# One queue for loads and stores: moving seven stores from ScalarE's DMA queue to SP's in a 1D Lp pooling kernel

## The chip, the cores and the metric

The kernel runs on one core of one Trainium2 chip. The metric is the device time of one execution in microseconds (us). All runs quoted are of state fast, and the granted clock was 1.00 in all of them.

Some words used throughout:

- A *load* brings x into on-chip memory, a *store* writes results back. Both are DMA transfers of 128 rows.
- A transfer is carried out by 16 DMA engines, 8 rows each. The trace records every row (here called a row or packet) with start and duration, and for each transfer 16 completions, one per DMA engine. The Trainium skill, page "DMA: Bandwidth & Descriptors", section "Why a DMA increments its semaphore by 16 and not by 1", says that the participating engines finish independently and that only the full 16 mean that all data has landed.
- A *ring* is what one DMA engine works off, in order, for one queue. The *lag* of a transfer is the last of its 16 completions minus the first. It is worked out from the trace's completion records, not printed by any view.
- A *slot* is a buffer of x; "slot 17's load" is the load of the eighteenth slot. A *turn* is the place in a ring where a store follows a load.

DVE is VectorE, ACT is ScalarE, POOL is GpSimd, SP is SyncE. A q after an engine's name means its sequencer, which issues transfers.

## The reference

```python
x: (32, 256, 4096) float32, p = 2.0, kernel_size = 4
for i in range(out_length):
    window = np.abs(x[:, :, 4*i:4*i+4]) ** p
    result[:, :, i] = np.mean(window, axis=-1) ** (1.0 / p)
```

With p = 2 this is the square root of the mean of four neighbouring squares. 134.22 MB are read and 33.55 MB written.

## The kernel before

All data is treated as one flat array, cut into rows over 128 partitions. Three slots for x (52,736 bytes per partition each) and two output buffers (26,368 bytes) rotate. Each of the groups 0 to 8 is two slots (groups 9 and 10 share the last two); the result of a group is one store. ScalarE squares a chunk, VectorE sums groups of four, ScalarE takes the root of the chunk before.

```python
    W, O_W = 13184, 6592
    X_SLOTS, O_SLOTS = 3, 2
    slots = [[(W, [4416, 4384, 4384])]] * 18
    slots += [[(6592, [3296, 3296])] * 2, [(6592, [3296, 3296]), (5056, [2528, 2528])]]
    groups = [2] * 9 + [3, 1]
    late = {7, 8, 9, 10}          # stored at the end, by SP
    in_x = {9, 10}                # these results go to a free slot of x
    # ... cut: bookkeeping, load(i) issues nc.sync.dma_start ...

    def store(g, queue):
        queue.dma_start(out=block(of, g, k), in_=ots[g])

    def root(g, o, ends):
        nc.scalar.activation(out=o, in_=o, func=Act.Sqrt, scale=1.0 / k)
        if ends and g not in late:
            store(g, nc.scalar)   # groups 0 to 6
    # ... cut ...
    for i in range(n):
        s, _, w, chunks = loads[i]
        while ahead < n and loads[ahead][0] < s + X_SLOTS:
            load(ahead)           # two slots ahead of the compute
            ahead += 1
        # ... cut: tiles ...
        for step in chunks:
            nc.scalar.activation(out=v, in_=v, func=Act.Square)
            nc.vector.tensor_reduce(out=o, in_=v.rearrange("p (n j) -> p n j", j=k), ...)
            if pending is not None:
                root(*pending)
            # ... cut ...
    for g in sorted(late):
        store(g, nc.sync)
```

Of the kernel before, what the change touches and what calls it, by code (L numbers as in the profile page):

```python
# [1 line left out]

# [4 lines left out]


@with_exitstack
def kernel(  # L10
    ctx: ExitStack,
    tc: tile.TileContext,
    x: bass.AP,
    p: float,
    kernel_size: int,
    out: bass.AP,
):






    nc = tc.nc

    assert float(p) == 2.0, "kernel specialized for p == 2"
    k = int(kernel_size)
    assert k == 4, "kernel specialized for kernel_size == 4"

    P = nc.NUM_PARTITIONS  # L30
    fp32 = mybir.dt.float32
    Act = mybir.ActivationFunctionType
    xf = x.rearrange("b c l -> (b c l)")
    of = out.rearrange("b c l -> (b c l)")
    total = xf.shape[0] // P
# [5 lines that stand above are left out]
    groups = [2] * 9 + [3, 1]  # L41
    late = {7, 8, 9, 10}
    in_x = {9, 10}


    loads = [(s, sum(w for w, _ in slot[:j]), *slot[j]) for s, slot in enumerate(slots)
             for j in range(len(slot))]
    n = len(loads)
    assert sum(w for _, _, w, _ in loads) == total

    firsts = [sum(groups[:g]) for g in range(len(groups))]
    assert sum(groups) == n
    group_of = [g for g, count in enumerate(groups) for _ in range(count)]
    columns = [sum(w for _, _, w, _ in loads[firsts[g]:firsts[g] + groups[g]])
               for g in range(len(groups))]

    x_pool = ctx.enter_context(tc.tile_pool(name="x_pool", bufs=X_SLOTS))
    o_pool = ctx.enter_context(tc.tile_pool(name="o_pool", bufs=O_SLOTS))
    ctx.enter_context(tc.manual_schedule())

    def block(flat, g, div):
        at, width = sum(columns[:g]) * P // div, columns[g] * P // div
        return flat[at:at + width].rearrange("(p w) -> p w", p=P)

    slot_tiles = {}
    xs = {}

    def load(i):
        s, at, w, _ = loads[i]
        if at == 0:  # L70
            slot_tiles[s] = x_pool.tile([P, W], fp32, name="xt")
        v = slot_tiles[s][:, at:at + w]
        g = group_of[i]
        src = sum(loads[j][2] for j in range(firsts[g], i))
        nc.sync.dma_start(out=v, in_=block(xf, g, 1)[:, src:src + w])  # L75
        xs[i] = v

    ots = {}

    def store(g, queue):  # L80
        queue.dma_start(out=block(of, g, k), in_=ots[g])  # L81

    def root(g, o, ends):
        nc.scalar.activation(out=o, in_=o, func=Act.Sqrt, scale=1.0 / k)  # L84
        if ends and g not in late:
            store(g, nc.scalar)

    ahead = 0
    while ahead < n and loads[ahead][0] < X_SLOTS - 1:
        load(ahead)  # L90
        ahead += 1
    pending = None
    for i in range(n):
        s, _, w, chunks = loads[i]
        while ahead < n and loads[ahead][0] < s + X_SLOTS:
            load(ahead)
            ahead += 1
        g = group_of[i]
        if i == firsts[g]:
            pool, width = (o_pool, O_W) if g not in in_x else (x_pool, W)  # L100
            t = pool.tile([P, width], fp32, name="ot" if g not in in_x else "xt")
            ots[g] = t[:, 0:columns[g] // k]
        at = sum(loads[j][2] for j in range(firsts[g], i)) // k
        assert sum(chunks) == w
        c = 0
        for step in chunks:
            v = xs[i][:, c:c + step]
            nc.scalar.activation(out=v, in_=v, func=Act.Square)  # L108
            o = ots[g][:, at + c // k:at + (c + step) // k]
            nc.vector.tensor_reduce(  # L110
                out=o, in_=v.rearrange("p (n j) -> p n j", j=k),
                axis=mybir.AxisListType.X, op=mybir.AluOpType.add,
            )
            if pending is not None:
                root(*pending)
            c += step
            pending = (g, o, i == firsts[g] + groups[g] - 1 and c == w)
    root(*pending)
    for g in sorted(late):
        store(g, nc.sync)  # L120


# [1 line left out]
_INS = ['x', 'p', 'kernel_size']  # L124
_OUTS = [((32, 256, 1024), 'float32')]

_NUMBERS = {'p': 2.0, 'kernel_size': 4}


# [26 lines left out]
```

## Time and profile before

| | before |
|---|---|
| time, median of 6 runs | 394.80 us (394.69 to 395.12) |
| span of the profiled run | 393.0 us |
| DVE / ACT busy | 72% / 74% |
| DMA, two queues together | 99.3% of 16 engines' span |
| row of a load / of a store | 1,947 ns / 978 ns (median of the row records) |

Lines of the page of the kernel before. The DMA line gives tenths of busy time in 40 slices of the span; a queue line gives packets, MB and the share of sixteen engines' span. The line of the sums ends with DVE's idle time before them; the last two give the transfers of one kind, KB each, and the median us from issue to landing.

```profile
span 393.0 us, 316 instructions
DVE 282.4 (72%) x62; ACT 292.4 (74%) x126; POOL 0.2 (0%) x4
...
DMA  8999999999999999999999999999999999999997
...
q1 hardware_dynamic: 3744, 144.15, 85.3%
q10 hardware_dynamic: 1008, 23.63, 14.0%
...
DMA 62%; ACT 19%; DVE 14%; issue 2%; ACTq 0%; SPq 0%
...
L110 DVE TENSOR_REDUCE ot<-xt 128x1096 f32<-128x4384 f32 (+1 forms) x54 | 255.4, 4731 | 102.7 <-ACT xt L108 102.4
...
xt<-in_x_dram SPq DMA_DIRECT2D x18, 6592.0 KB, 39.7
out_dram<-ot ACTq DMA_DIRECT2D x7, 3296.0 KB, 26.4
```

No compute engine is near full, and the DMA engines are full from the first microseconds to the last: the kernel is bound by DMA. Queue q1 is SP's (loads and the four late stores), q10 ScalarE's (seven stores).

Who waits for whom, in the kernel before (total us, times, longest):

```profile
DVE ot L110 <- ACT xt L108: 102.4, 36, 23.4
...
ACT xt L108 <- DMA xt<-in_x_dram: 86.3, 18, 17.5
```

Compute waits for loads only, never for a store. In the timeline, at slot 4 and at the end (start, duration, engine, line, operation):

```profile
90.41 3.88 ACT L108 ACTIVATE xt<-xt 128x4416 f32<-128x4416 f32 x1 [4.84 <-DMA xt<-in_x_dram]
94.32 4.75 DVE L110 TENSOR_REDUCE ot<-xt 128x1104 f32<-128x4416 f32 x1 [5.01 <-ACT xt L108]
...
339.75 3.88 ACT L108 ACTIVATE xt<-xt 128x4416 f32<-128x4416 f32 x1 [1.07 <-DMA xt<-in_x_dram]
...
381.39 6.11 SPq L81 DMA_DIRECT2D out_dram<-xt  x2
...
386.42 0.73 ACT L84 ACTIVATE xt<-xt 128x632 f32<-128x632 f32 x1 [2.23 <-DVE xt L110]
```

Slot 4's load has landed by 90.4 us, slot 17's by 339.75 us; from there ACT and DVE run almost without a break to 387 us, and the last two stores are issued at 381.4 and 387.2 us.

### The profile page before, as it was taken

How to read it: one execution, taken by the hardware profiler on the slowest of the kernel's cores; microseconds unless marked ns; L12 is line 12 of the kernel's file. 1: busy time of each engine (PE TensorE's matmuls, PEld its weight loads, DVE VectorE, ACT ScalarE, POOL GpSimd, SP SyncE). 2: the span in 40 equal slices, each digit the busy share in tenths (PEclk: the TensorE clock that was granted, in tenths of full speed). 3: DMA queues.
4: the chain of work that ended last, by engine and by line, in shares of the span. 5: the costliest groups of instructions: out<-in, count | busy, mean ns of one | idle time of the engine just before them, and what ended most of it. 6: DMA issues, size and time to landing. Idle time of an engine off the chain costs nothing.

```text
span 393.0 us, 316 instructions
## 1 busy us (share of the span) xinstructions
DVE 282.4 (72%) x62; ACT 292.4 (74%) x126; POOL 0.2 (0%) x4
## 2 busy tenths in 40 slices
DVE  0068989494959495949594959595859686899992
ACT  1099986777786768686958695959595949899991
POOL 0000000000000000000000000000000000000000
DMA  8999999999999999999999999999999999999997
GB/s 344 429 429 440 429 424 381 443 459 429 413 440 435 429 427 432 429 440 441 437 448 421 432 462 435 392 429 472 429 413 451 425 429 429 424 429 427 438 429 329
DMA packets 4754, 167.79 MB, mean 427 GB/s; under 512 B 528, under 2 KB 528, under 8 KB 656
## 3 DMA queue, kind: packets, MB, share of 16 engines
q1 hardware_dynamic: 3744, 144.15, 85.3%
q10 hardware_dynamic: 1008, 23.63, 14.0%
q14 instruction: 2, 0.02, 0.0%
HBM read 134.22 MB, written 33.55 MB: 427 GB/s over the span
## 4 chain that ended last, share of the span: by engine, by line
DMA 62%; ACT 19%; DVE 14%; issue 2%; ACTq 0%; SPq 0%
DMA xt<-in_x_dram 62%; ACT xt L108 15%; DVE ot L110 11%; DVE xt L110 3%; ACT ot L84 3%; ACT xt L84 1%; ACTq L81 0%; SPq L75 0%; ACTq L108 0%
## 5 line engine op out<-in xcount | busy, mean ns | idle before, releaser
L110 DVE TENSOR_REDUCE ot<-xt 128x1096 f32<-128x4384 f32 (+1 forms) x54 | 255.4, 4731 | 102.7 <-ACT xt L108 102.4
L108 ACT ACTIVATE xt<-xt 128x4384 f32<-128x4384 f32 (+3 forms) x62 | 230.3, 3716 | 89.2 <-DMA xt<-in_x_dram 86.3
L84 ACT ACTIVATE ot<-ot 128x1096 f32<-128x1096 f32 (+1 forms) x54 | 59.8, 1108 | 1.8 <-DVE ot L110 0.9
L110 DVE TENSOR_REDUCE xt<-xt 128x824 f32<-128x3296 f32 (+1 forms) x8 | 27.0, 3384 | 1.3 <-ACT xt L108 1.2
L84 ACT ACTIVATE xt<-xt 128x824 f32<-128x824 f32 (+1 forms) x8 | 6.7, 841 | 3.0 <-DVE xt L110 2.9
L108 ACT ACT_TABLE_LOAD x1 | 1.3, 1283 | 0.7 <-PEq L137 0.7
L84 ACT ACT_TABLE_LOAD x1 | 1.3, 1283 | 0.0
L137 POOL MEMSET const-bfloat16-1.0<- 128x1 bf16 x1 | 0.1, 101 | 0.0
L137 POOL MEMSET const-uint8-127<- 128x1 uint8 x1 | 0.1, 101 | 0.0
L137 POOL MEMSET const-float32-0.0<- 128x1 f32 x1 | 0.1, 98 | 0.2 <-issue 0.2
L137 POOL MEMSET const-float32-1.0<- 128x1 f32 x1 | 0.1, 98 | 0.0
## 6 DMA issues: line engine op xcount, KB each, us to landing
xt<-in_x_dram SPq DMA_DIRECT2D x18, 6592.0 KB, 39.7
out_dram<-ot ACTq DMA_DIRECT2D x7, 3296.0 KB, 26.4
xt<-in_x_dram SPq DMA_DIRECT2D x3, 3296.0 KB, 24.6
out_dram<-ot SPq DMA_DIRECT2D x2, 3296.0 KB, 29.6
xt<-in_x_dram SPq DMA_DIRECT2D x1, 2528.0 KB, 26.4
out_dram<-xt SPq DMA_DIRECT2D x1, 2472.0 KB, 9.3
out_dram<-xt SPq DMA_DIRECT2D x1, 632.0 KB, 5.0
```

The costliest lines, as they stand in the source:

```text
L84: nc.scalar.activation(out=o, in_=o, func=Act.Sqrt, scale=1.0 / k)
L108: nc.scalar.activation(out=v, in_=v, func=Act.Square)
L110: nc.vector.tensor_reduce(out=o, in_=v.rearrange("p (n j) -> p n j", j=k), axis=mybir.AxisListType.X, op=mybir.AluOpType.add,)
L137: nc = _bacc.Bacc("TRN2", target_bir_lowering=False, num_devices=1)
```

## The change

The intent is to issue all stores from SP's queue, in turn with the loads, and none from ScalarE. The rewritten bookkeeping (FINE, LAG) at the values given here leaves the order of the squares, sums and roots as it was. What is left of the change is one word:

```diff
@@
     in_x = {9, 10}
+    FINE, LAG = 0, 1
@@
         nc.scalar.activation(out=o, in_=o, func=Act.Sqrt, scale=1.0 / k)
         if ends and g not in late:
-            store(g, nc.scalar)
+            store(g, nc.sync)
@@ (cut: the same passes, with a list of pending roots)
+            while pending and pending[0][0] <= done - LAG:
+                root(*pending.pop(0)[1:])
```

In SP's order a store now stands behind the load of two slots ahead: load, load, store, load, load, store.

More of the change, by code (lines that the diff above doesn't have):

```diff
@@ L85, in root, with total_sum @@
         if ends and g not in late:
-            store(g, nc.scalar)
+            store(g, nc.sync)
+    def total_sum(o, v, i):
+        nc.vector.tensor_reduce(
+            out=o, in_=v.rearrange("p (n j) -> p n j", j=k),
+            axis=mybir.AxisListType.X, op=mybir.AluOpType.add,
+        )
     ahead = 0
@@ L91 @@
         ahead += 1
-    pending = None
+    pending = []
+    done = 0
     for i in range(n):
@@ L102 @@
             ots[g] = t[:, 0:columns[g] // k]
-        at = sum(loads[j][2] for j in range(firsts[g], i)) // k
+            summed = rooted = 0
         assert sum(chunks) == w
@@ L108 @@
             nc.scalar.activation(out=v, in_=v, func=Act.Square)
-            o = ots[g][:, at + c // k:at + (c + step) // k]
-            nc.vector.tensor_reduce(
-                out=o, in_=v.rearrange("p (n j) -> p n j", j=k),
-                axis=mybir.AxisListType.X, op=mybir.AluOpType.add,
-            )
-            if pending is not None:
-                root(*pending)
-            c += step
-            pending = (g, o, i == firsts[g] + groups[g] - 1 and c == w)
-    root(*pending)
+            total_sum(ots[g][:, summed:summed + step // k], v, i)
+            while pending and pending[0][0] <= done - LAG:
+                root(*pending.pop(0)[1:])
+            done += 1
+            c += step
+            summed += step // k
+            ends = summed == columns[g] // k
+            if ends or i >= FINE:
+                pending.append((done - 1, g, ots[g][:, rooted:summed], ends))
+                rooted = summed
+    for job in pending:
+        root(*job[1:])
     for g in sorted(late):
```

## The prediction

> **What bounds the kernel now.** The DMA engines. In the page's slices the DMA row reads 9 nearly everywhere; DVE is busy 72% and ACT 74% of the span. The queue lines give 85.3% (loads and last stores) plus 14.0% (ScalarE's stores) = 99.3% of sixteen engines' span of 393.0 us. In the packet records one engine's packets sum to 390.1 us; the first starts at 1.7 us, the last ends at 391.7: no gaps. A load row (52,736 bytes) takes 1,947 ns and a store row (26,368 bytes) 978 ns, alone or beside the other queue: sharing costs no bandwidth. The chain of waits agrees: 62% DMA loads.
>
> **What the change does.** The order of ACT's and DVE's passes stays. It removes seven store issues from ACT (0.34 us each, on an engine 26% idle) and adds them to SP, each behind the load two slots ahead. No load should wait behind a store: each store is ready before the next load in SP's order, whose slot still has reductions to run.
>
> What moves is the order inside the rings. Before, store and load rows alternate when both queues hold work (the Trainium skill, "DMA: Bandwidth & Descriptors", section Queues, rings and completion order: round-robin at packet granularity); 26 us from issue to landing for a store that needs 7.8 us alone (8 x 978 ns) agrees. After, one ring runs in order: load, load, store. My estimate from 15.6 us per load and 7.8 per store: the first load of a group lands about 8 us earlier (slot 4 near 82 us instead of 90.4), the store behind it near 90. Stores take 34 to 43 us to land instead of 26.
>
> With two output buffers, the first reduction of group g waits for the store of g-2. Now the load comes last; after, the store: DVE waits for it some 4 us after the first squaring, seven times. But that reduction starts 3 to 4 us earlier than now (about 90.4 against 94.3 in slot 4), since load plus store are the same bytes. Loads keep their lead: each is issued some 20 us before its turn.
>
> **The tail.** Bytes ahead of slot 17's load are the same, so it lands near 339.7 us as now; slot 16 is reduced some 4 us earlier. From there ACT and DVE run without a break to 387 us, and the four late stores stay on SP. Group 9's store is issued at 381.4, the one before lands at 384.8: about a microsecond to spare after start-up, a little more after. The end stays with the rings.
>
> **Predicted time.** Head 1.7 + packets 390.1 + landing and end 1.2 = 393.0 us of span, 394.7 us measured (now 394.79). There is nothing to win; only a gap could cost. Range 394.1 to 396.0. Faster by over 2%: 0.01, within 2%: 0.96, slower by over 2%: 0.03.
>
> **What would show each step.** Queue 1 carries all 167.8 MB at 99%; packet times unchanged; store issue to landing about 40 us; DVE's or ACT's idle before the first chunk of groups 2 to 8 ends with a store; load issue to landing 35 to 40 us; no wait of SP for a store's data that empties the ring.
>
> **What would make it wrong.** A gap in the ring at each change from load to store (at 1 us each, up to 14 us); a waiting store holding a load until the ring runs dry; slot 16's reduction gated so late by group 6's store that the compute tail outlasts the stores: several us more.

## The result, and the profile after

| | before | after |
|---|---|---|
| time, median of 6 runs | 394.80 us (394.69 to 395.12) | 397.11 us (396.80 to 397.23) |
| ratio | | 1.0057, 95% interval 1.0044 to 1.0070 |
| span of the profiled run | 393.0 us | 395.3 us |
| mean of the 16 rings' packet time | 390.1 us | 390.7 us |
| end of the last packet | 391.7 us | 394.0 us |
| lag of slot 17's load | 0.94 us | 3.34 us |

A ratio is the mean time of one kernel's fast runs over that of the other's fast runs of the same rounds, so it is not quite the ratio of the medians quoted.

The change costs 2.3 us (0.6%): within 2%, but outside the predicted range (394.1 to 396.0), and clear of the noise.

Lines of the page after:

```profile
span 395.3 us, 330 instructions
DVE 281.7 (71%) x62; ACT 291.8 (74%) x126; POOL 0.2 (0%) x4
...
DMA  8999999989999999999999999999999999999996
...
q1 hardware_dynamic: 4752, 167.77, 98.8%
...
DMA 67%; ACT 15%; DVE 15%; issue 0%; SPq 0%; DVEq 0%; ACTq 0%
...
L90 DVE TENSOR_REDUCE ot<-xt 128x1096 f32<-128x4384 f32 (+1 forms) x54 | 254.7, 4729 | 105.7 <-ACT xt L116 67.0
...
xt<-in_x_dram SPq DMA_DIRECT2D x18, 6592.0 KB, 37.4
out_dram<-ot SPq DMA_DIRECT2D x9, 3296.0 KB, 41.8
```

There is one queue now. The DMA line looks full as before, with an 8 near 80 us and a 6 at the end. Stores take 41.8 us to land instead of 26.4, since they queue behind two loads.

The waits after (the last line is of SP's own waits, shown by a view of its own):

```profile
DVE ot L90 <- ACT xt L116: 67.0, 29, 23.6
ACT xt L116 <- DMA xt<-in_x_dram: 64.4, 18, 17.7
DVE ot L90 <- DMA out_dram<-ot: 38.7, 7, 6.6
...
SPq L76 <- DVE ot L90: 292.2, 17, 18.6
```

A new wait stands here: seven times DVE waits for a store to free the output buffer. It is tempting to call these 38.7 us the cause. But 102.4 us of waiting for ACT became 67.0 (and the wait of ACT for loads fell from 86.3 to 64.4): DVE's idle time before these sums is 105.7 us after against 102.7 before. The timeline shows the same:

```profile
83.68 3.88 ACT L116 ACTIVATE xt<-xt 128x4416 f32<-128x4416 f32 x1 [2.57 <-DMA xt<-in_x_dram]
91.51 4.75 DVE L90 TENSOR_REDUCE ot<-xt 128x1104 f32<-128x4416 f32 x1 [6.65 <-DMA out_dram<-ot]
...
326.55 9.38 DVE L90 TENSOR_REDUCE ot<-xt 128x1104 f32<-128x4416 f32 x2 [5.43 <-DMA out_dram<-ot]
...
342.07 3.88 ACT L116 ACTIVATE xt<-xt 128x4416 f32<-128x4416 f32 x1 [4.85 <-DMA xt<-in_x_dram]
...
383.73 6.12 SPq L82 DMA_DIRECT2D out_dram<-xt  x2
...
388.75 0.73 ACT L85 ACTIVATE xt<-xt 128x632 f32<-128x632 f32 x1 [2.23 <-DVE xt L90]
```

In slot 4 the sum starts at 91.5 us, earlier than before (94.3). But slot 17 starts at 342.07 instead of 339.75 us, 2.3 us later, behind a load, and everything after it is later by the same amount.

The completions tell why. First and last of the 16 completions (us), from the trace's records:

```
                       before                    after
slot 4's load       89.55   90.38 (0.83)      81.57   83.60 (2.03)
slot 6's load      128.47  129.32 (0.86)     120.52  123.07 (2.54)
slot 8's load      167.39  168.24 (0.85)     159.47  162.40 (2.94)
slot 12's load     245.24  246.06 (0.82)     237.43  240.32 (2.89)
slot 17's load     338.72  339.67 (0.94)     338.64  341.99 (3.34)
store of group 8   383.81  384.76            383.74  387.07
store of group 9   389.70  390.66            390.84  392.97
store of group 10  391.25  392.22            392.39  394.53
```

The first ring to complete slot 17's load is as early as before (338.64 against 338.72); the last is 2.3 us later. At the end, the last completions follow one another at 5.90 and 1.56 us, which is 8 rows of 735 ns and 8 of 194 ns: the ring that is last works without a pause. The first completions of groups 8 and 9 are 7.10 us apart where 8 rows need 5.88: those rings had run dry, because the next store was not yet issued (383.73 us, when the first ring was already done with group 8's). So the sixteen rings have drifted apart, and the end is set by the one that is last.

The row records show where. Of the rows of 1,947 ns that start after 50 us, those stretched by more than 100 ns are, after the change: 17 at 77.8 to 80.3 us, directly ahead of the first store, and one at 91.1 (16.9 us of stretch together, about 1 us for every ring); then 25 more in small sets of 1 to 8 to the end, all but three of them just before one of the stores 1 to 6 begins (7.9 us together, up to 0.83 us in one row). Before the change there are 29 between 56 and 62 us, at the first store (15.7 us together, again about 1 us per ring), and then two in the whole rest. These two (at 178.0 and 310.3 us), and two of the three exceptions after the change (175.0 and 307.8), start as a packet of 309 ns of queue q14, named "instruction" on the page, ends. Such a pair stands in both kernels, so it does not explain their difference.

### The profile page after: what moved, and what is told of

It reads as the page before. It is cut to its first block, busy times and chain, and to the rows that moved or that the text cites. A ratio compares the mean times of both kernels' runs of the same rounds, so it can differ in the third digit from the quotient of the medians.

```text
span 395.3 us, 330 instructions
## 1 busy us (share of the span) xinstructions
DVE 281.7 (71%) x62; ACT 291.8 (74%) x126; POOL 0.2 (0%) x4
## 3 DMA queue, kind: packets, MB, share of 16 engines
q1 hardware_dynamic: 4752, 167.77, 98.8%
## 4 chain that ended last, share of the span: by engine, by line
DMA 67%; ACT 15%; DVE 15%; issue 0%; SPq 0%; DVEq 0%; ACTq 0%
DMA xt<-in_x_dram 46%; DMA out_dram<-ot 21%; ACT xt L116 12%; DVE ot L90 12%; DVE xt L90 3%; ACT ot L85 2%; ACT xt L85 1%; SPq L76 0%; DVEq L90 0%; ACTq L116 0%
## 5 line engine op out<-in xcount | busy, mean ns | idle before, releaser
L90 DVE TENSOR_REDUCE ot<-xt 128x1096 f32<-128x4384 f32 (+1 forms) x54 | 254.7, 4729 | 105.7 <-ACT xt L116 67.0
L116 ACT ACTIVATE xt<-xt 128x4384 f32<-128x4384 f32 (+3 forms) x62 | 230.3, 3716 | 64.4 <-DMA xt<-in_x_dram 64.4
## 6 DMA issues: line engine op xcount, KB each, us to landing
xt<-in_x_dram SPq DMA_DIRECT2D x18, 6592.0 KB, 37.4
out_dram<-ot SPq DMA_DIRECT2D x9, 3296.0 KB, 41.8
```

## The experiments

*Theory A*: at a turn from a load to a store inside one ring, load rows in flight are stretched, not equally in all rings; a ring that falls behind never catches up, because it is never idle; the last ring sets the landing of slot 17's load and the end. *Rivals*: B, one event at the first store; C, with two queues the rings even out again; D, the waits for output buffers (compute); E, the compute tail that starts late, rather than the ring.

Every kernel was run in 5 rounds against the kernel before on the same chip; there were two chips, one for d_one, d_two, e_tail_light and e_warm_before, the other for the rest. Each run's lag is that of its one profiled execution. Where two queues are at work, the lag of the odd slots' loads is in some runs about 1 us larger than that of the even ones and gone at the next slot (e_first_sp: 3.14 at slot 13, 2.17 at slot 14). That is about one store row (978 ns), so it is probably the place in the alternation and not a drift; therefore only even slots and slot 17, behind the last of the seven stores, are compared.

### c_after: the changed kernel again

> The changed kernel again, on the chip of the next three, as a control. In the first profile the 16 completions of one DMA (one per ring) spread over 0.95 us before the change and 3.3 us after it by slot 17's load, and the span grew by 2.3 us. If this belongs to the kernel, it comes back: ratio about 1.006, spread of slot 17's load 3 to 3.5 us. If it was a matter of that one execution or chip, the spread is another and the time follows it.

No edit. Measured: 396.65 us against 394.76, ratio 1.0049 (1.0035 to 1.0062); lag of slot 17's load 2.69 us. It comes back smaller, 1.9 us instead of 2.3, with a lag below the expected 3 to 3.5. Its row records show one thing more: 14 stretched rows (5.1 us together) at 128.3 to 132.4 us, when store 1 ended and the next load began. The lag hardly changed there (2.23 us at slot 6, 2.28 at slot 7). So rows are not stretched only ahead of a store, and not every stretch adds lag.

### e_first_sp: only store 0 by SP

```diff
-            store(g, nc.sync)
+            store(g, nc.sync if g == 0 else nc.scalar)
```

> Only store 0 goes by SP, stores 1 to 6 by ScalarE as before. Theory A (each turn from a load to a store inside one ring stretches load rows, and a ring that fell behind never catches up): store 0's turn took the spread from 1.3 to 2.0 us, so about +0.7 to +1.2 us on before (395.5 to 396.0) and a spread that stays near 2.0. Rival B (the first store alone does it, by a single event on all rings near 78 us): nearly all of the 2.3 us (397). Rival C (with two queues the rings even out again): as before (394.8), spread back to 0.9.

Measured: 396.12 us against 394.76, ratio 1.0032 (1.0020 to 1.0045), lag 2.17 us. C (394.8) falls. B's 397 was not reached, but the changed kernel itself took only 396.65 on this chip, so this one store made 1.4 of its 1.9 us; that B is not the whole is shown by e_rest_sp. A's time came out 0.1 us above its range, and one detail does not fit A: slot 4's load, ahead of the SP store, had a lag of 1.58 us (slot 2's had 1.13), and the step to 2.07 (slot 6's load) came with stretched rows at 95 to 97 us, beside the rows of the first ScalarE store, which began at 91.5. So half of the growth came with two queues at work and not at a turn. From slot 8 on the lag stays from 2.15 to 2.27 at every even slot, to the end. So with two queues the lag does not grow after the first ScalarE store, but it does not shrink either.

### e_rest_sp: store 0 by ScalarE, stores 1 to 6 by SP

```diff
-            store(g, nc.sync)
+            store(g, nc.scalar if g == 0 else nc.sync)
```

> Store 0 by ScalarE, stores 1 to 6 by SP. Theory A: the spread starts at 0.85 us and grows by the share of stores 1 to 6 in the changed kernel (1.3 us): about +1.3 us (396.1). Rival B: as before (394.8 to 395.1), spread flat at 0.9. Rival D (any in-order ring beside compute loses time evenly, by DMA waits at the output buffers): +2.0 (6/7 of the whole) without growth of the spread.

Measured: 396.52 us against 394.76, ratio 1.0039 (1.0027 to 1.0052). The lag of the loads directly ahead of the stores was 0.94 (slot 6), 1.07, 1.63, 1.98, 2.20 and 2.49 us (slot 16). It grows turn by turn, without the first store's event. This is A's pattern, with a time 0.4 us over its figure; B as the whole cause is out, and so is D's flat lag. But the parts do not add up: 1.36 us (e_first_sp) and 1.76 us (this run) make 3.12, where the whole change made 1.89 on the same chip. That fits a lag that stops growing near 3 us (next run), and the step of e_first_sp that was no turn.

### e_two_apart: twice as many turns

Each group is stored in two halves, one behind each load, all by SP.

```diff
-        if ends and g not in late:
-            store(g, nc.sync)
+        if ends is not None and g not in late:
+            store(g, nc.sync, ends)      # ends: which half of the columns
```

> All stores by SP, but each in two halves, one behind each load: 14 turns from load to store in place of 7, the same bytes. Theory A: the spread grows more, 4 to 5.5 us, and the time by another 1 to 2.5 us over the changed kernel (398 to 399.5). Rival D (the waits at the output buffers): the halves land earlier, so less DVE waiting for stores and a time nearer to before (395 to 396.5). Rival B: as the changed kernel (397).

Measured: 396.94 us against 394.76, ratio 1.0055 (1.0042 to 1.0067). A's size was missed: the time is that of the changed kernel, which is what B had forecast. The lag speaks against B and shows why the time grew no further: 1.49, 1.83, 2.47, 2.59, 2.90 us at the loads of slots 3 to 7, so it grows at every turn, and faster per group than in the changed kernel; then it stays between 2.8 and 3.0 us to the end (2.96 at slot 17). The growth stops by itself near 3 us. Why it stops is not settled.

### d_one and d_two: the transfers with hardly any compute

Both keep the transfers and all waits, but each pass works on 64 columns of its chunk, and GpSimd fills the output tiles first; output wrong. d_one stores by SP, d_two by ScalarE. A build of each, without the fill, would have stored memory that nothing had written.

```diff
-            nc.scalar.activation(out=v, in_=v, func=Act.Square)
-            total_sum(ots[g][:, summed:summed + step // k], v, i)
+            nc.scalar.activation(out=v[:, 0:64], in_=v[:, 0:64], func=Act.Square)
+            total_sum(ots[g][:, summed:summed + 16], v[:, 0:64], i)
```

> Transfers as in the changed kernel, all stores by SP in the same order, but each pass works on 64 columns of its chunk only (output wrong on purpose; GpSimd fills the output tiles with ones first). Theory A (load rows stretched at each turn from load to store in the ring, lag of a ring kept): the lag grows as in the changed kernel, to 2.5 to 3.3 us, and the time stays at 396.2 to 397.2 though there is hardly any compute. Rival D (waits of DVE and ACT at the output buffers, or the compute tail, make it slower): 394.8 or less.

> The same with stores 0 to 6 by ScalarE. Theory A: lag flat near 0.9 us, 394.3 to 394.9, so some 2 us under d_one. Rival D: the same as d_one.

Page of d_one:

```profile
span 395.2 us, 368 instructions
DVE 12.8 (3%) x62; ACT 23.1 (6%) x126; POOL 55.8 (14%) x15
...
q1 hardware_dynamic: 4752, 167.77, 98.9%
```

Page of d_two:

```profile
span 392.8 us, 347 instructions
DVE 13.5 (3%) x62; ACT 23.9 (6%) x126; POOL 55.8 (14%) x15
...
q1 hardware_dynamic: 3744, 144.15, 85.3%
q10 hardware_dynamic: 1008, 23.63, 14.0%
```

Measured: d_one 396.97 us, ratio to before 1.0050 (1.0036 to 1.0064), lag of slot 17's load 2.93 us. d_two 394.68 us, ratio 0.9996 (0.9984 to 1.0009), lag 0.99 us. The same 2.3 us lie between one queue and two when DVE and ACT are busy 3% and 6% of the span. Rival D is out, and the 395 us are the DMA's alone in both kernels.

### e_tail_light: a short compute tail

In slots 18 and 19 of the changed kernel, square and sum are replaced by one short DVE pass; output wrong there.

```diff
+            if s < 18:
                 (square and sum as before)
+            else:
+                nc.vector.tensor_scalar_max(
+                    ots[g][:, summed:summed + step // k], v[:, 0:step // k], 0.0)
```

> The changed kernel, but in the last loads (slots 18 and 19) the square and the reduction are replaced by one short DVE pass over a quarter of the columns (output wrong on purpose in these columns), so the compute after slot 17 ends more than 10 us earlier and the last two stores are issued early. If the ring that lags sets the end itself (Theory A): unchanged against the changed kernel, 396.3 to 397.2, with the late stores of the lagging ring back to back. Rival E (the lag only matters because the compute tail of 47 us starts late, so that the last stores are issued late): 394.8 to 395.3.

From its timeline, the last roots and the issue of the last two stores:

```profile
367.35 5.99 SPq L82 DMA_DIRECT2D out_dram<-xt  x2
371.11 0.89 DVE L120 TENSOR_SCALAR xt<-xt 128x632 f32<-128x632 f32 x2 [4.99 <-DMA xt<-in_x_dram]
371.63 1.35 ACT L85 ACTIVATE xt<-xt 128x632 f32<-128x632 f32 x2 [4.31 <-DVE xt L120]
```

Measured: 396.65 us against 394.81, ratio 1.0043 (1.0031 to 1.0056), lag 2.78 us. The last stores were issued 16 us earlier than in the changed kernel, and the time stayed within the 396.65 and 397.11 us of that kernel's two measurements (neither is on record as made on this chip). E falls: the ring that is last sets the end by itself. In the changed kernel the compute tail ends late too, but it is not what holds the end.

### e_warm_before: a small first store

The kernel before plus a store of 128 rows of 512 bytes at the very start.

```diff
+    nc.vector.memset(warm, 0.0)
+    nc.scalar.dma_start(out=block(of, 10, k)[:, 0:128], in_=warm)
     ahead = 0
```

> The kernel before plus one small store (128 rows of 512 bytes of zeros, by ScalarE at the very start, overwritten by the last store). In both kernels every ring lost about 1 us around the first store of the execution (two load rows of some 2.45 us in the first ScalarE store of before, one of some 2.95 us ahead of the first SP store after). If that is the cost of the first store of an execution, whichever it is, the small one takes it while the rings start up: 393.6 to 394.3. If it is the cost of the first large store, or of the first turn under full load: 394.8 to 395.0.

Measured: 394.95 us against 394.81, ratio 1.0001 (0.9989 to 1.0014), so nothing was won. The rows at 57 to 62 us were stretched as before. The microsecond that every ring loses at the first large store is not taken by a small one at the start, when nothing else is in flight. What it is remains open; it is in both kernels, so it does not explain their difference.

### e_half_after and e_half_before: load rows of half the length

```diff
-        nc.sync.dma_start(out=v, in_=block(xf, g, 1)[:, src:src + w])
+        for c in range(0, w, w // 2):
+            nc.sync.dma_start(out=v[:, c:c + w // 2],
+                              in_=block(xf, g, 1)[:, src + c:src + c + w // 2])
```

> The changed kernel with each load issued as two, left and right half of the columns: rows of 26,368 bytes (978 ns) in place of 52,736 (1,947 ns), the same bytes and the same number of turns. In the runs so far the lag stopped growing at 2.7 to 3.3 us, 1.4 to 1.7 times a load row's time, and only the last row of a load ahead of a store was stretched. If the stretch and the limit go with the row in flight at the turn (Theory A1): lag of slot 17's load at most 2.0 us, 395.2 to 396.0. If they do not depend on the row (Theory A2): 2.5 to 3.3 us, 396.3 to 397.2.

> The kernel before with the same halved loads, as the control of e_half_after: the halving itself should cost nothing, 394.5 to 395.3, lag under 1.5 us. Were it 396 or more, halving costs by itself and e_half_after says nothing.

Measured: e_half_after 396.45 us against 394.87, ratio 1.0038 (1.0025 to 1.0050); e_half_before 396.67, ratio 1.0046 (1.0032 to 1.0060). The control missed: halving costs by itself. The rings' mean packet time is 391.8 us with one queue and 391.9 with two, 1.7 us more than in the kernel before, for 176 more rows per ring. But rows that follow one another overlap by about 3 ns in the records, so this sum counts too much: the last packet of e_half_before ended at 392.79 us, 1.1 us later than before the change (391.72) at the same lag, which is about 6 ns a row. Another 0.5 us of its span came after the last landing, where SP's last waits took longer (its span ended 1.32 us after that landing, 0.79 in the kernel before). By my own condition the times say nothing about A1 and A2. The lag can still be read: 1.84 us (slot 17's last half) with one queue and 0.91 with two, so it is smaller than with full rows (2.7 to 3.3), as A1 expected. But it was still growing at the last turn (1.52 to 1.81), so this shows a slower growth and not a limit. With halved rows the two arrangements are level in time, within the noise. In the profiled runs the last landing was 0.5 us later with one queue (393.80 against 393.28 us), and the longer end of e_half_before made that up, so a difference of that size may be hidden here.

### e_pool: the stores by GpSimd's queue

```diff
-            store(g, nc.sync)
+            store(g, nc.gpsimd)
```

> Stores 0 to 6 by GpSimd's queue, loads and late stores by SP. Theory A (only a turn inside the loads' own ring lets the lag grow; any second queue avoids it): 394.5 to 395.4, lag flat and under 2.2 us. If ScalarE's queue is what does it: as the changed kernel, 396.3 to 397.3. GpSimd's issues may be slower than the 0.34 us of ScalarE's, but hide behind idle time.

Measured: 395.73 us against 394.87, ratio 1.0020 (1.0007 to 1.0032), lag 1.95 us. The lag is 1.95 to 1.98 at each even slot from slot 4 to 16, that is, one step at the first store and then flat, as A expects of any second queue. The time is 0.3 us over A's range, because that one step was upward here (1.10 to 1.95), where in the kernel before it was downward (1.27 to 0.83). The step at the first store of a second queue thus differs from kernel to kernel, and why is open. A second queue does not save the 2 us by itself: of them e_pool still lost 0.9.

### All runs on one line each

Lag of slot 17's load and span of the same profiled run (full-length load rows only):

| run | queue of stores 0 to 6 | lag, us | span, us |
|---|---|---|---|
| before | ACT | 0.94 | 393.0 |
| d_two | ACT | 0.99 | 392.8 |
| e_warm_before | ACT | 1.62 | 393.5 |
| e_pool | POOL | 1.95 | 394.0 |
| e_first_sp | SP once, then ACT | 2.17 | 394.1 |
| e_rest_sp | ACT once, then SP | 2.48 | 394.7 |
| c_after | SP | 2.69 | 394.9 |
| e_tail_light | SP | 2.78 | 394.9 |
| d_one | SP | 2.93 | 395.2 |
| e_two_apart | SP, halves | 2.96 | 395.2 |
| after | SP | 3.34 | 395.3 |

Eleven different executions, with full compute and with hardly any: a microsecond of lag is about a microsecond of span. From the first to the last row it is 2.3 us of span for 2.4 us of lag. The bytes are the same throughout (e_warm_before has 64 KB more).

## Why the prediction was wrong

- *DMA is the bound; the order of passes stays; compute waits for stores but is not later for it*: right. DVE's new wait for stores (seven times; in slot 4 it ended 4.0 us after the first squaring, predicted some 4), slot 4's landing (83.6, predicted near 82), its store (91.4, predicted near 90), a store's way to landing (41.8, predicted about 40) and the loads' (37.4, predicted 35 to 40) came as said. Slot 4's sum did start 2.8 us earlier (predicted 3 to 4).
- *No load is held behind a waiting store, no gap in the ring*: right up to the tail. The queue line shows 98.8%, and the last ring is without a pause to the end. The tail's "about a microsecond to spare" was used up: with slot 17 2.3 us late, group 9's store came after the first ring was done with group 8's, and the leading rings stood still. As e_tail_light shows, that did not set the end.
- *"In the packet records one engine's packets sum to 390.1 us"*, and from it *"Head 1.7 + packets 390.1 + landing and end 1.2"*: this is the step that failed. 390.1 us was the mean over the sixteen rings, taken for each of them. The term that counts is the way of the ring that is last, from the first packet's start to the last one's end: 390.0 us before and 392.3 after (1.75 to 394.02), where the prediction kept 390.1. The mean grew only from 390.1 to 390.7. So 0.6 us of the 2.3 is packet time added on average, and the other 1.7 is what the last ring lost beyond the mean. That the mean fitted the kernel before was partly luck: by my estimate the overlaps of 3 ns, over 297 records of a ring, put 0.9 us too much into it, about what the last ring's lag of 0.94 us hides.
- *"Bytes ahead of slot 17's load are the same, so it lands near 339.7 us as now"*: failed for the same reason. The bytes are the same and the first ring is on time (338.64 us); the load landed at 341.99.
- *"alone or beside the other queue: sharing costs no bandwidth"*: the median row shows this in both kernels (1,947 and 978 ns). A median can't show a few tens of stretched rows among 2,304. They were in the records before too, 29 at the first store, and were passed over.
- *"at 1 us each, up to 14 us"*: among the dangers named, this was the nearest. The turn does cost, but it stretches rows instead of leaving gaps, by some tenths of a microsecond for the ring that is last, and the sum stops near 3 us of lag.

Shown by the runs: the cost is in the DMA rings and not in compute (d_one, d_two); with one queue the lag grows at the turns (e_rest_sp, e_two_apart, the row records); with two it steps, down or up, at the first store of the second queue and is flat at the even slots afterwards (before, e_first_sp, e_pool); the ring that is last sets the end (e_tail_light, and the table). Not shown, and left open: why a load row that is in flight when a store begins in the same queue is stretched, while with two queues load and store rows alternate for hundreds of microseconds without it; why the lag stops near 3 us; what sets the step at the first store of a second queue (0.4 us down in the kernel before, 0.85 up in e_pool); and what the first large store costs a microsecond for.

No version beat the kernel before by more than the noise. d_two, with hardly any compute, was level with it, so the compute of the kernel before is hidden entirely.

## What to carry to other kernels

When DMA is the bound, look at the sixteen completions of a transfer, not only at the mean busy share: in these runs' streams without pauses a ring that fell behind stayed behind, and the kernel ended with it. Here it was worth 0.6% to keep stores in ScalarE's queue (GpSimd's queue kept part of that: a ratio of 1.0020 instead of 1.0057), although bytes, median row times and engines were the same. Don't read a new wait in the profile as the cause before an experiment that removes it: DVE's 38.7 us of waiting for stores were not the cause: d_one, with DVE busy 3% of the span, was as slow.

## What the Trainium skill lacked or had wrong

- "DMA: Bandwidth & Descriptors", section "Issuing engines are not separate DMA queues", says that issuing from several engines only saves the sequencer's time to issue. Here one queue against two made 2.3 us of 395 with next to no compute (d_one 396.97, d_two 394.68), and SP's queue was no bottleneck (after the change it waited 292.2 us for DVE to free slots). The measurement decides: in a saturated stream the split over queues can matter by 0.6%.
- The same page, "Queues, rings and completion order", explains that rings are separate and that packets of two queues alternate; in the trace of the kernel before, load and store rows alternate one by one (97 to 118 us), and the store's 26.4 us to landing instead of 8 rows of 978 ns agrees. It does not say that the rings of one queue drift apart at turns from loads to stores and stay so: a lag of 0.94 us against 2.7 to 3.3.
- The same page, "Specifications", gives about 27 GiB/s per DMA engine. Rows of 52,736 bytes took 1,947 ns here, which is 27.1 GB/s, or 25.2 GiB/s.
- The same page has no figure for a large row's being cut in two: about 6 ns a row here (the last packet 1.1 us later for 176 more rows per ring, e_half_before).
- No page has the stretch of load rows at the first large store of an execution: about 1 us per ring (16 to 17 us over the sixteen) in both kernels.
